# The state-space layer of a two-layer diffusion backbone: modulation sums in the other PSUM bank pair, back-rotations and transposes in other places

## The chip, the cores and the metric

The kernel runs on one core of a Trainium2 chip. The metric is the device time of one execution in microseconds (us). [...] Each engine takes its own instructions in order and waits at semaphores for the others.

## The reference

Two trunk layers run over 1024 latent tokens and 256 context tokens of width 1024. Layer 0 mixes tokens with differential attention, layer 1 with a bidirectional S5 state space; each mixer is followed by a squared-ReLU MLP, with RMS norms and modulation (shift, scale, gate) from `SiLU(c)` before and after. The change lies in layer 1's mixer:

```
def step(h, uc):
    bu = einsum('gpc,btgc->btgp', b_bar, uc)
    a_cum, hs = associative_scan(_linear_combine, (a, bu), axis=1)
    hs = hs + a_cum * h[:, None]
    y = real(einsum('gcp,btgp->btgc', c_mat, hs))
...
y = y_forward + y_backward[:, ::-1] + d_skip * h
g = gelu(y);  o1, o2 = split(g @ w_glu, 2);  out = o1 * sigmoid(o2)
```

There are 64 groups of 16 channels with 64 complex states each, scanned in both directions. The layer's modulation is `mod = SiLU(c) @ ada_w[1] + ada_b[1]`, a vector of six segments of 1024 for each of the two streams.

## The kernel before, in words

The program (class `Prog`) runs in stages: attention, output projection, MLP of layer 0, the state-space stage `s5()`, the gated linear unit `glu()`, and the MLP of layer 1. Most of the stages are ordered by a scheduler that estimates when each instruction is due. The main loop of `s5()` is written under `manual()`: TensorE, VectorE, ScalarE and GpSimd take their instructions in the order of the Python text. Only SyncE's DMA queue is still ordered by the scheduler.

Before the stage, token time is cut in chunks of 8 tokens, so that a scan runs over 160 chunks (32 of context, 128 of latent tokens). One step `n` of the loop (0 to 15) treats four groups of channels in both directions `d`:

- `inputs(n, d)` (L1765): 16 matmul calls into `xbank[d]`, the chunk inputs of the states. The two `xbank`s span PSUM banks 0 to 2 and share bank 1.
- `phase(n, d)` (L1744, GpSimd): adds two integer tables to the phases of the rotation; `trig(n, d)` (L1749 to L1753, ScalarE): five instructions make sines `Ps` and cosines `Pc` of them. The three phase buffers are used in turn, so `phase(n+1, 1)` writes where the sines of `(n, 0)` are, and `phase(n+1, 0)` where those of `(n-1, 1)` are.
- `rotate(n, d)` (L1774, VectorE, two instructions): multiplies `xbank[d]` by cosines (`t1`) and sines (`t2`); GpSimd adds the two (L1878 for `d` = 0, L1886 for `d` = 1). This turns the complex scan into real ones.
- `decay(n, d)` (L1779, ScalarE): fills `r`, in PSUM, with the decay; `scan(n, d)` (L1784, VectorE): two scans, over the two parts `c`, each of 320 elements.
- `back(engine, n, d, j)` (L1793): the rotation back, `j` = 0 with cosines and `j` = 1 with sines. For each direction VectorE does `j` = 0 and GpSimd `j` = 1.
- `outputs(n)`: `lags` (L1809), the terms inside a chunk, and `products` (L1817), the states times the output matrices, into `ypart(n, i)`. It is called one step later, as `outputs(n - 1)` in step `n`.
- For step `m = n - 2`, the GELU: square (L1860, ScalarE, reads `ybank(n)`), L1874 (VectorE), tanh (L1875), plus one (L1880), and the product with `y` (L1894, VectorE).
- `tr` (L1827): transposes of the result into `ypart(n, i)`; `tr_out`: ScalarE copies it rounded (L1832), VectorE stores the residue (L1833). Products in this kernel use such pairs of a rounded value and its residue.

`ybank(n)` is the pair of banks 4 and 5 for even `n`, 6 and 7 for odd `n`. `ypart(n, i)` takes the first half of each 256 elements; the second half is used by `accum(n, i)`, for the modulation. The framework sets its waits by whole banks: a matmul that writes a bank waits for readers of any part of it, and the other way round.

The modulation of layer 1, segments 2 to 5, is made in this stage in eight halves of 512 columns. List `mods` holds a triple (a, b, buffers) for each: in step a the weights are loaded (`ada_half_load`, four DMAs of 512 KB), in step b `ada_half_products` (L270) multiplies them into `accum(n)`, 64 rows of the profile, in step b + 1 ScalarE copies the sums (L1863), `ada_half_columns` (L274) transposes them into `accum(n, 1)`, and in step b + 2 `ada_half_add` (L279, L281, L284, VectorE) adds them to the table of modulations. Seven halves have b = 3, 5, ... 15; the eighth has b = 12.

Three more steps (16 to 18) finish outputs, GELU and transposes. Then `glu()` splits its weights (L137, L138) and multiplies (L132 to L134).

Of the kernel before, what the change touches and what calls it, by code (L numbers as in the profile page):

```python
# [9 lines left out]
AF = mybir.ActivationFunctionType  # L10
ALU = mybir.AluOpType
# [59 lines left out]
class Prog:  # L71
# [1627 lines left out]
    def s5(self):  # L1699
# [4 lines left out]
        v, act, pool, mm = nc.vector, nc.scalar, nc.gpsimd, nc.tensor.matmul  # L1704
# [8 lines left out]
        phs = [(self.fv(x, 2, 2, 160), self.fv(x + 2.5, 2, 160)) for x in (0, 7.5, 24.5)]  # L1713
        ts = [[(self.fv(x, 2, 2, 160), self.fv((12.5, 20)[d], 2, 2, 160)) for x in ((5, 29.5), (15, 17.5))[d]] for d in range(2)]
        cs = [[(self.fv(x, 2, 2, 128), self.fv(y, 2, 2, 128)) for x, y in (((5, 32), (29.5, 34)), ((15, 22.5), (17.5, 22.5)))[d]]
              for d in range(2)]
# [7 lines left out]

        extra = [self.view(self.U, 56, (2, 512)), self.fv(49, 2, 512), self.fv(53, 2, 512), self.wv(10, 2, 512)]
        early = [self.view(self.U, 4 * kk, (2, 512)) for kk in range(4)]
        mods = [(2 * i + 1, 2 * i + 3, extra) for i in range(7)] + [(8, 12, early)]

        def load_x(n):
            self.dma(slots[n % 2][3][:, 0:1024] if n else x_first, self.recd[n, :, 0:1024])  # L1730
# [9 lines left out]
        def phase(n, d):  # L1740

            x0, P = 32 * d + 2 * n, phs[(2 * n + d) % 3][0][:, 1].bitcast(I32)
            a, b = (At[:, x0 : x0 + 2], Bt[:, x0 : x0 + 2]) if n else (A0[:, d], B0[:, d])
            pool.tensor_tensor(P.rearrange("p x (a b) -> p x a b", b=16), bcast(a, 3, 16), bcast(b, 2, 10), ALU.add)  # L1744

        def trig(n, d):
            Ps, Pc = phs[(2 * n + d) % 3]
            P = Ps[:, 1].bitcast(I32)
            act.activation(Pc, P, AF.Sin, scale=0.5 * UNPHASE)  # L1749
            act.activation(Ps[:, 0], P, AF.Sin, scale=-UNPHASE)  # L1750
            act.activation(Ps[:, 1], P, AF.Sin, scale=UNPHASE)
            act.activation(Pc, Pc, AF.Square, scale=float(np.sqrt(2.0)))
            act.activation(Pc, Pc, AF.Copy, bias=-1.0)  # L1753
# [3 lines left out]
        def inputs(n, d):  # L1757
            X = slots[n % 2][0] if n else shaped(x_first, (2, 4, 128))
            cols = slice(0, 160) if d == 0 else slice(32, 192)
            for c in range(2):  # L1760
                for y in range(2):
                    o = 176 * (2 * c + y)
                    for h in range(2):
                        i = 2 * h + y
                        mm(xbank[d][64 * h : 64 * h + 64, o : o + 160], X[:, d, i, 64 * c : 64 * c + 64],  # L1765
                           U[:, 4 * n + i, cols], start=True, stop=True)

        def rotate(n, d):
            (Ps, Pc), (t1, t2) = phs[(2 * n + d) % 3], ts[d][n % 2]
            b = xbank[d]  # L1770
            for j, t in enumerate((t1, t2)):
                x = bass.AP(b.tensor, b.offset + (159 if d else 0) + 352 * j,
                            [list(b.ap[0]), [-352 if j else 352, 2], [176, 2], [-1 if d else 1, 160]])
                v.tensor_tensor(t, x, Ps if j else bcast(Pc, 1, 2), ALU.mult)  # L1774

        def decay(n, d):

            x0 = 32 * d + 2 * n
            act.activation(rx[:, :, 1:160], bcast(r8[:, x0 : x0 + 2], 2, 159), AF.Copy)  # L1779

        def scan(n, d):
            for c in range(2):
                t1, t2 = (t[:, c].rearrange("p x n -> p (x n)") for t in ts[d][n % 2])
                v.tensor_tensor_scan(t2, r, t1, 0.0, ALU.mult, ALU.add)  # L1784

        def back(eng, n, d, j):
            Ps, Pc = phs[(2 * n + d) % 3]
            o = cs[d][n % 2][j]
            if d:
                o = bass.AP(o.tensor, o.offset + 127, [list(o.ap[0]), [256, 2], [128, 2], [-1, 128]])  # L1790
            h = slice(31, 159)
            t2 = ts[d][n % 2][1][:, :, :, h]
            eng.tensor_tensor(o, t2, Ps[:, :, :, h] if j else bcast(Pc[:, :, h], 1, 2), ALU.mult)  # L1793
# [8 lines left out]
        def accum(n, i=0):  # L1802
            x = 2176 + 1024 * (n % 2) + 256 * i
            return self.PS[:, x : x + 128]
# [24 lines left out]
        def tr_out(kb, g, n):  # L1829
            b = ybank(n, (1, 128))  # L1830
            hi, lo = (shaped(gT[g][j][:, kb], (4, 128)) for j in range(2))
            act.activation(hi, b, AF.Copy, scale=0.5)  # L1832
            v.scalar_tensor_tensor(lo, b, 0.5, hi.bitcast(F32), ALU.mult, ALU.subtract)  # L1833
# [8 lines left out]
        with self.manual():  # L1842
            act.activation(U[:, :, 160:192], U[:, :, 0:32], AF.Copy)
            v.memset(rx[:, :, 0:1], 0.0)
            phase(0, 0)
            phase(0, 1)
            trig(0, 0)
            decay(0, 0)
            inputs(0, 0)
            inputs(0, 1)  # L1850
            load_x(1)
            load_w(1)
            for n in range(19):
                run, m = n < 16, n - 2
                gelu = 0 <= m < 16
                y, uf = ybank(n, (1, 128)), u.rearrange("p i t c -> p i (t c)")
                if 1 <= n <= 16:
                    back(pool, n - 1, 1, 1)
                if gelu:
                    act.activation(uf, y, AF.Square, scale=float(np.sqrt(0.044715)))  # L1860
                for a, b, w in mods:
                    if n == b + 1:
                        act.activation(self.adat[:, 0:128], accum(b), AF.Copy)  # L1863
                if run:
                    trig(n, 1)
                if 0 < n < 15:
                    phase(n + 1, 0)
                if run:
                    rotate(n, 0)
                for i, (a, b, w) in enumerate(mods):  # L1870
                    if n == b + 2:
                        self.ada_half_add(1, 2 + i // 2, i % 2, accum(n - 1, 1))
                if gelu:
                    v.scalar_tensor_tensor(uf, uf, 1.0, y, ALU.add, ALU.mult)  # L1874
                    act.activation(u, u, AF.Tanh, scale=float(np.sqrt(2.0 / np.pi)))  # L1875
                if run:
                    t1, t2 = ts[0][n % 2]
                    pool.tensor_tensor(t1, t1, t2, ALU.add)  # L1878
                if gelu:
                    act.activation(u, u, AF.Copy, bias=1.0)  # L1880
                if 0 < n < 15:
                    trig(n + 1, 0)
                if run:
                    rotate(n, 1)
                    t1, t2 = ts[1][n % 2]
                    pool.tensor_tensor(t1, t1, t2, ALU.add)  # L1886
                    scan(n, 0)
                    if n == 0:
                        phase(1, 0)
                        trig(1, 0)  # L1890
                    decay(n, 1)
                if gelu:
                    gv = ggs[m // 2 % 2].rearrange("p t g c -> p g t c")
                    v.tensor_tensor(gv[:, 4 * (m % 2) : 4 * (m % 2) + 4], u, ybank(n, (16, 8), (1, 16)), ALU.mult)  # L1894
                if run:
                    back(v, n, 0, 0)
                    back(pool, n, 0, 1)
                    scan(n, 1)
                    back(v, n, 1, 0)
                if n < 15:  # L1900
                    decay(n + 1, 0)
                if 1 <= n <= 16:
                    outputs(n - 1)
                if n < 15:
                    inputs(n + 1, 0)
                    inputs(n + 1, 1)
                if n + 1 < 16:
                    phase(n + 1, 1)
                if 3 <= n < 19:
                    tr((n - 3) // 2, 1 - n % 2, n)  # L1910
                    tr_out((n - 3) // 2, 1 - n % 2, n)
                for a, b, w in mods:
                    if n == b:
                        self.ada_half_products(w, accum(n))
                    if n == b + 1:
                        self.ada_half_columns(accum(n, 1))
                if n + 2 < 16:
                    load_x(n + 2)
                if 1 <= n and n + 1 < 16:
                    load_w(n + 1)  # L1920
                for i, (a, b, w) in enumerate(mods):
                    if n == a:
                        self.ada_half_load(w, 1, 2 + i // 2, i % 2)
# [402 lines left out]
```

## Time and profile before

| | |
|---|---|
| median of 3 runs | 2949.05 us (2947.05 to 2949.87) |
| profiled execution | 2948.53 us |
| its span | 2946.7 us |
| first `scan(0, 0)`, from the span's start | 1918.11 us |
| `scan(3, 0)` | 1947.28 us |
| `scan(15, 0)` | 2102.45 us |
| first matmul of `glu()` | 2127.05 us |
| mean granted TensorE clock | 0.981 |

In the rows of the profile, L12 is line 12 of the kernel. A group gives busy time, the mean of one instruction in ns, and the idle time of its engine just before it with what ended that. A row of the timeline gives start and length in us, engine, line, what is written and read, the count merged, and in brackets the idle time ahead and who ended it; where the engine named had long been done, it was another. The clock is a share of full speed.

### The profile page before, as it was taken

The numbers are of one execution on the slowest core, as the hardware profiler recorded it, in microseconds if no ns is written. First come the engines' busy times: TensorE is split into PE (matmuls) and PEld (weight loads), VectorE is DVE, ScalarE is ACT, GpSimd is POOL, SyncE is SP. The second block draws the span as 40 slices with busy tenths as digits, with TensorE's granted clock in tenths as the row PEclk, the third lists the DMA queues.
The fourth block names the chain that finished last, engine by engine and source line by source line (L and its number), as shares of the span: only waits on it lengthen the run. The fifth ranks groups of instructions, "written<-read, shape, count | busy, mean of one in ns | idle before, by whom it ended". The sixth has DMA issues, their size and how long they took to land.

```text
span 2946.7 us, 45520 instructions
## 1 busy us (share of the span) xinstructions
PE 2789.1 (95%) x16556; PEld 2300.8 (78%) x16556; DVE 1909.2 (65%) x2823; ACT 1304.4 (44%) x2476; POOL 990.9 (34%) x911
## 2 busy tenths in 40 slices
PE   7999999999899999999999999687799999999999
PEld 5687888888777877888777788576688778888887
DVE  5456888888764654444687754787633676659466
ACT  3325565555544743333432222355434655345443
POOL 2214667667653500000000002476301323327324
PEclk9999999999899999999999999889899999999999
DMA  9964444454716455322666653656534475467544
GB/s 265 296 193 159 136 157 154 147 154 156 239 59 187 136 159 169 121 97 88 211 191 187 181 158 95 170 182 184 178 115 154 149 228 188 150 214 268 161 136 140
DMA packets 404493, 494.42 MB, mean 168 GB/s; under 512 B 41014, under 2 KB 279596, under 8 KB 403372
## 3 DMA queue, kind: packets, MB, share of 16 engines
q1 hardware_dynamic: 403884, 489.42, 53.0%
q8 instruction: 130, 2.13, 0.3%
q10 hardware_dynamic: 384, 2.10, 0.3%
q14 instruction: 95, 0.78, 0.1%
HBM read 337.77 MB, written 149.43 MB: 165 GB/s over the span
## 4 chain that ended last, share of the span: by engine, by line
PE 66%; DVE 12%; DMA 7%; issue 6%; ACT 6%; POOL 2%; SPq 1%; DVEq 0%; ACTq 0%; POOLq 0%
PE PS L132 20%; PE PS L134 19%; PE PS L133 19%; ACT F L574 2%; DVE F L564 2%; PE PS L539 2%; PE PS L597 1%; DVE FD L1784 1%; DVE R L138 1%; SPq L80 1%; PE PS L208 1%; PE PS L1817 1%; DVE FD L1774 1%; DMA W<-in_mlp_w 1%; DVE FD L1675 1%
## 5 line engine op out<-in xcount | busy, mean ns | idle before, releaser
L132 PE MATMUL PS<-H,R 128*128 128x512 f32 (+1 forms) x816 | 301.8, 372 | 8.7 <-DVE FC L490 5.5
L132 PE MATMUL PS<-H 128*128 128x512 f32 x768 | 300.1, 392 | 3.6 <-ACT H L137 2.3
L133 PE MATMUL PS<-H 128*128 128x512 f32 x768 | 299.4, 390 | 0.0
L134 PE MATMUL PS<-H 128*128 128x512 f32 x768 | 298.7, 390 | 0.0
L133 PE MATMUL PS<-H,R 128*128 128x512 f32 (+1 forms) x816 | 293.3, 359 | 1.4 <-POOL H L138 1.4
L134 PE MATMUL PS<-H,R 128*128 128x512 f32 (+1 forms) x816 | 293.2, 360 | 0.0
L132 PE MATMUL PS<-R,H 128*128 128x512 f32 x540 | 216.7, 403 | 1.9 <-ACT R L137 1.6
L574 ACT ACTIVATE F<-F,stat 128x1280 f32<-128x1280 f32 x128 | 174.3, 1362 | 98.8 <-DVE F L564 98.5
L137 ACT ACTIVATE R<-W 128x512 fp32r<-128x512 f32 (+1 forms) x184 | 131.1, 717 | 189.7 <-PE PS L133 136.0
L133 PE MATMUL PS<-R,H 128*128 128x512 f32 x540 | 212.1, 393 | 0.0
L134 PE MATMUL PS<-R,H 128*128 128x512 f32 x540 | 211.6, 395 | 0.0
L138 DVE TENSOR_TENSOR H<-W,H 128x512 fp32r<-128x512 f32 (+1 forms) x145 | 136.5, 946 | 99.0 <-ACT H L137 93.5
L564 DVE TENSOR_SCALAR_CACHE_REDUCE F<-PS 128x1280 f32<-128x1280 f32 x128 | 185.1, 1482 | 14.1 <-PE PS L539 14.0
L138 DVE TENSOR_TENSOR R<-W,R 128x512 fp32r<-128x512 f32 (+1 forms) x148 | 126.3, 858 | 98.2 <-ACT R L137 77.8
L611 POOL TENSOR_SCALAR R<-F 128x256 fp32r<-128x256 f32 (+1 forms) x128 | 137.2, 1072 | 147.8 <-ACT F L610 134.4
L132 PEld LDWEIGHTS PS<-H,R 128*128 128x128 f32 x816 | 154.2, 189 | 38.8 <-DVE FC L490 7.2
L137 ACT ACTIVATE H<-W 128x512 fp32r<-128x512 f32 (+2 forms) x166 | 107.4, 653 | 170.6 <-PE PS L133 117.1
L539 PE MATMUL PS<-R,R 64*128 64x256 f32 (+1 forms) x1440 | 159.1, 349 | 16.6 <-DVE F L564 9.9
L134 PEld LDWEIGHTS PS<-H,R 128*128 128x128 f32 x816 | 154.2, 189 | 26.3 <-POOL R L138 1.4
L132 PEld LDWEIGHTS PS<-H 128*128 128x128 f32 x768 | 144.1, 188 | 37.1 <-ACT H L137 3.1
L133 PEld LDWEIGHTS PS<-H,R 128*128 128x128 f32 x816 | 154.6, 189 | 22.5 <-POOL H L138 1.6
L134 PEld LDWEIGHTS PS<-H 128*128 128x128 f32 x768 | 144.2, 188 | 30.2 <-issue 0.2
(460 smaller groups left out, 7172.7 us busy)
## 6 DMA issues: line engine op xcount, KB each, us to landing
W<-in_mlp_w SPq DMA_DIRECT2D x192, 256.0 KB
Ad<-F SPq DMA_DIRECT2D x112, 256.0 KB
W<-Ad SPq DMA_DIRECT2D x112, 256.0 KB
W<-in_ada_w SPq DMA_DIRECT2D x41, 512.0 KB
W<-in_mlp_w SPq DMA_DIRECT2D x32, 512.0 KB
H<-hidd SPq DMA_DIRECT2D x64, 256.0 KB
W<-in_s_w_glu SPq DMA_DIRECT2D x64, 256.0 KB
hidd<-FU SPq DMA_DIRECT2D x52, 256.0 KB
```

The lines of the kernel that those rows point to most:

```text
L80: return self.nc.sync.dma_start(out=out, in_=in_)
L132: mm(out, ah, bh, start=first, stop=False, **kw)
L133: mm(out, ah, bl, start=False, stop=False, **kw)
L134: mm(out, al, bh, start=False, stop=last, **kw)
L137: self.nc.scalar.activation(hi, src, AF.Copy)
L138: (lo_eng or self.nc.vector).tensor_tensor(lo, src, hi.bitcast(F32), ALU.subtract)
L208: self.nc.tensor.matmul(acc[32 * j : 32 * j + 32, 0:256], self.scT[:, 2 * k : 2 * k + 32], w[:, 256 * j : 256 * j + 256], start=k == 0, st ...
L539: mm(self.PS[:, o : o + k1 - k0], Q[rows, i, qs], K[j][rows, k0:k1], start=n == 0, stop=n == 2)
L564: ts(p[c], self.PS[:, 1280 * c : 1280 * c + 1280], 1.0, None, ALU.mult, ALU.min, accum_out=sm[:, c : c + 1])
L574: nc.scalar.activation(p[c], p[c], AF.Exp, bias=sm[:, c : c + 1], scale=-1.0, accum_out=sn[:, 0:1] if c else s0[:, u + 1 : u + 2])
L597: self.nc.tensor.transpose(tb[:, 128 * (kt - k0) : 128 * (kt - k0) + 128], w[:, 128 * kt : 128 * kt + 128], self.ident)
L611: nc.gpsimd.tensor_scalar(hi, t, 1.0, 0.0, ALU.mult, ALU.add)
```

## The change

- The modulation products of step b go into `accum(n - 1)`, the bank pair of the other parity; the copy, the transpose and the add follow (`accum(b - 1)`, `accum(n - 1, 1)`, `accum(n - 2, 1)`). On TensorE the transpose and the products now come after both `inputs`, in this order.
- The eighth half has b = 16 in place of 12, and its loads are in step 14 in place of 8.
- In ScalarE's order, `trig(n, 1)` comes ahead of the square and the copy of the sums; `decay(n + 1, 0)` comes after `tr_out`'s copy.
- The back-rotations change hands: GpSimd does `j` = 0, VectorE `j` = 1. VectorE's first stands between the two scans of direction 1, its second, of the step before, between the two halves of `rotate(n, 0)`.
- On GpSimd, the order stays: back-rotation, phase, addition, addition, back-rotation, phase. The two phase additions overwrite sines that VectorE's back-rotations now read.
- On TensorE the transposes come between `inputs(n + 1, 0)` and `inputs(n + 1, 1)`, which were together ahead of them.

```diff
@@ -1724,7 +1724,7 @@
 
         extra = [self.view(self.U, 56, (2, 512)), self.fv(49, 2, 512), self.fv(53, 2, 512), self.wv(10, 2, 512)]
         early = [self.view(self.U, 4 * kk, (2, 512)) for kk in range(4)]
-        mods = [(2 * i + 1, 2 * i + 3, extra) for i in range(7)] + [(8, 12, early)]
+        mods = [(2 * i + 1, 2 * i + 3, extra) for i in range(7)] + [(14, 16, early)]
 
         def load_x(n):
             self.dma(slots[n % 2][3][:, 0:1024] if n else x_first, self.recd[n, :, 0:1024])
@@ -1765,10 +1765,11 @@
                         mm(xbank[d][64 * h : 64 * h + 64, o : o + 160], X[:, d, i, 64 * c : 64 * c + 64],
                            U[:, 4 * n + i, cols], start=True, stop=True)
 
-        def rotate(n, d):
-            (Ps, Pc), (t1, t2) = phs[(2 * n + d) % 3], ts[d][n % 2]
+        def rotate(n, d, js=(0, 1)):
+            Ps, Pc = phs[(2 * n + d) % 3]
             b = xbank[d]
-            for j, t in enumerate((t1, t2)):
+            for j in js:
+                t = ts[d][n % 2][j]
                 x = bass.AP(b.tensor, b.offset + (159 if d else 0) + 352 * j,
                             [list(b.ap[0]), [-352 if j else 352, 2], [176, 2], [-1 if d else 1, 160]])
                 v.tensor_tensor(t, x, Ps if j else bcast(Pc, 1, 2), ALU.mult)
@@ -1778,8 +1779,8 @@
             x0 = 32 * d + 2 * n
             act.activation(rx[:, :, 1:160], bcast(r8[:, x0 : x0 + 2], 2, 159), AF.Copy)
 
-        def scan(n, d):
-            for c in range(2):
+        def scan(n, d, cs=(0, 1)):
+            for c in cs:
                 t1, t2 = (t[:, c].rearrange("p x n -> p (x n)") for t in ts[d][n % 2])
                 v.tensor_tensor_scan(t2, r, t1, 0.0, ALU.mult, ALU.add)
 
@@ -1855,28 +1856,30 @@
                 gelu = 0 <= m < 16
                 y, uf = ybank(n, (1, 128)), u.rearrange("p i t c -> p i (t c)")
                 if 1 <= n <= 16:
-                    back(pool, n - 1, 1, 1)
+                    back(pool, n - 1, 1, 0)
+                if run:
+                    trig(n, 1)
                 if gelu:
                     act.activation(uf, y, AF.Square, scale=float(np.sqrt(0.044715)))
                 for a, b, w in mods:
                     if n == b + 1:
-                        act.activation(self.adat[:, 0:128], accum(b), AF.Copy)
+                        act.activation(self.adat[:, 0:128], accum(b - 1), AF.Copy)
                 if run:
-                    trig(n, 1)
+                    rotate(n, 0, (0,))
+                if 1 <= n <= 16:
+                    back(v, n - 1, 1, 1)
                 if 0 < n < 15:
                     phase(n + 1, 0)
                 if run:
-                    rotate(n, 0)
+                    rotate(n, 0, (1,))
+                    t1, t2 = ts[0][n % 2]
+                    pool.tensor_tensor(t1, t1, t2, ALU.add)
                 for i, (a, b, w) in enumerate(mods):
                     if n == b + 2:
-                        self.ada_half_add(1, 2 + i // 2, i % 2, accum(n - 1, 1))
+                        self.ada_half_add(1, 2 + i // 2, i % 2, accum(n - 2, 1))
                 if gelu:
                     v.scalar_tensor_tensor(uf, uf, 1.0, y, ALU.add, ALU.mult)
                     act.activation(u, u, AF.Tanh, scale=float(np.sqrt(2.0 / np.pi)))
-                if run:
-                    t1, t2 = ts[0][n % 2]
-                    pool.tensor_tensor(t1, t1, t2, ALU.add)
-                if gelu:
                     act.activation(u, u, AF.Copy, bias=1.0)
                 if 0 < n < 15:
                     trig(n + 1, 0)
@@ -1893,27 +1896,28 @@
                     gv = ggs[m // 2 % 2].rearrange("p t g c -> p g t c")
                     v.tensor_tensor(gv[:, 4 * (m % 2) : 4 * (m % 2) + 4], u, ybank(n, (16, 8), (1, 16)), ALU.mult)
                 if run:
-                    back(v, n, 0, 0)
-                    back(pool, n, 0, 1)
-                    scan(n, 1)
-                    back(v, n, 1, 0)
-                if n < 15:
-                    decay(n + 1, 0)
+                    back(pool, n, 0, 0)
+                    scan(n, 1, (0,))
+                    back(v, n, 0, 1)
+                    scan(n, 1, (1,))
+                if n + 1 < 16:
+                    phase(n + 1, 1)
                 if 1 <= n <= 16:
                     outputs(n - 1)
                 if n < 15:
                     inputs(n + 1, 0)
-                    inputs(n + 1, 1)
-                if n + 1 < 16:
-                    phase(n + 1, 1)
                 if 3 <= n < 19:
                     tr((n - 3) // 2, 1 - n % 2, n)
                     tr_out((n - 3) // 2, 1 - n % 2, n)
+                if n < 15:
+                    inputs(n + 1, 1)
+                    decay(n + 1, 0)
+                for a, b, w in mods:
+                    if n == b + 1:
+                        self.ada_half_columns(accum(n - 1, 1))
                 for a, b, w in mods:
                     if n == b:
-                        self.ada_half_products(w, accum(n))
-                    if n == b + 1:
-                        self.ada_half_columns(accum(n, 1))
+                        self.ada_half_products(w, accum(n - 1))
                 if n + 2 < 16:
                     load_x(n + 2)
                 if 1 <= n and n + 1 < 16:
```

## The prediction

> **What bounds the kernel now.** I read the page first: engine totals, slices, granted clock.
>
> ```profile
> span 2946.7 us, 45520 instructions
> PE 2789.1 (95%) x16556; PEld 2300.8 (78%) x16556; DVE 1909.2 (65%) x2823; ACT 1304.4 (44%) x2476; POOL 990.9 (34%) x911
> PE   7999999999899999999999999687799999999999
> PEclk9999999999899999999999999889899999999999
> ```
>
> TensorE (PE) is busy 95% of the span, so only places where it pauses can give time. The low digits (slices 24 to 29 of 40, 73.7 us each) hold the state-space stage, and the clock row dips at the same place. Next, stretches from one scan(n,0) start to another: steps 1 to 3, steps 3 to 15, and the tail from step 15 to the first gated-linear-unit matmuls; the last row is a small piece inside a step.
>
> ```profile
> core 0: us, PE busy (x) PEld busy (x) DVE busy (x) ACT busy (x) POOL busy (x), PEclk, DMA share, GB/s
> 1947.20:2102.40 155.20, 123.57 (x1723) 108.12 (x1721) 124.01 (x171) 86.00 (x199) 92.59 (x71) 0.91 0.61 194
> 1929.30:1947.20 17.90, 17.80 (x232) 16.13 (x232) 17.37 (x24) 12.09 (x28) 15.74 (x13) 0.94 0.65 180
> 2102.40:2127.00 24.60, 15.85 (x202) 13.26 (x198) 11.46 (x19) 7.43 (x14) 4.48 (x3) 0.84 0.49 152
> 2020.30:2023.70 3.40, 3.31 (x24) 3.08 (x26) 3.40 (x6) 3.02 (x7) 2.77 (x2) 0.51 0.11 38
> ```
>
> Columns: length, busy time and count of PE, PEld, DVE, ACT, POOL, then granted clock, DMA share, GB/s. Steps 3 to 15 are 12 steps in 155.2 us, 12.93 each, in which no engine is full: PE 123.6 us, VectorE (DVE) 124.0, ScalarE (ACT) 86.0, GpSimd (POOL) 92.6. So the steps are bound by waits between engines. Steps 1 to 3, without modulation sums, have DVE busy 17.37 of 17.90. The groups of those 12 steps:
>
> ```profile
> L1774 DVE TENSOR_TENSOR FD<-PS,FD 128x640 f32<-128x640 f32 x49 | 38.0, 815 | 14.4 <-ACT FD L1753 14.4
> L1784 DVE TENSOR_TENSOR_SCAN FD<-PS,FD 128x320 f32<-128x320 f32 x48 | 36.6, 801 | 0.0
> L1793 DVE TENSOR_TENSOR FD<-FD 128x512 f32<-128x512 f32 x24 | 26.0, 1084 | 0.4
> L1833 DVE SCALAR_TENSOR_TENSOR H<-PS,H 128x512 fp32r<-128x512 f32 x12 | 8.3, 692 | 12.8 <-ACT H L1832 12.8
> L284 DVE TENSOR_TENSOR modc<-modc,ng 128x8 f32<-128x8 f32 x5 | 3.7, 737 | 0.2
> L1863 ACT ACTIVATE adat<-PS 128x128 f32<-128x128 f32 x7 | 1.9, 278 | 18.2 <-DVE FD L1874 9.2 <-PE PS L270 6.4 <-PE PS L274 2.5
> ```
>
> Reading: scans (L1784, four a step) never waited; DVE stood 14.4 us ahead of rotations (L1774) for ACT's trigonometry, and 12.8 us ahead of the transpose residue (L1833) for ACT's copy L1832. The back-rotations (L1793) average 1084 ns. The copy of modulation sums (L1863) kept ACT waiting 18.2 us. One step in order of time:
>
> ```profile
> 2008.22 0.28 ACT L1863 ACTIVATE adat<-PS 128x128 f32<-128x128 f32 x1 [2.31 <-DVE FD L1874]
> 2010.62 1.55 DVE L1774 TENSOR_TENSOR FD<-PS,FD 128x640 f32<-128x640 f32 x2 [2.41 <-ACT FD L1753]
> 2011.13 0.63 ACT L1880 ACTIVATE FD<-FD 128x512 f32<-128x512 f32 x1
> 2011.67 0.45 ACT L1749 ACTIVATE FD<-FD 128x320 f32<-128x320 int32 x1
> 2012.09 1.53 DVE L1784 TENSOR_TENSOR_SCAN FD<-PS,FD 128x320 f32<-128x320 f32 x2
> 2013.75 0.42 ACT L1779 ACTIVATE PS<-r 128x318 f32<-128x318 f32 x1
> 2013.76 1.28 POOL L1793 TENSOR_TENSOR FD<-FD 128x512 f32<-128x512 f32 x1
> 2014.11 1.48 DVE L1793 TENSOR_TENSOR FD<-FD 128x512 f32<-128x512 f32 x1
> 2015.51 1.52 DVE L1784 TENSOR_TENSOR_SCAN FD<-PS,FD 128x320 f32<-128x320 f32 x2
> 2017.07 0.69 DVE L1793 TENSOR_TENSOR FD<-FD 128x512 f32<-128x512 f32 x1
> 2017.13 0.44 ACT L1779 ACTIVATE PS<-r 128x318 f32<-128x318 f32 x1 [2.96 <-DVE FD L1784]
> 2017.50 0.58 ACT L1832 ACTIVATE H<-PS 128x512 fp32r<-128x512 f32 x1
> 2017.98 0.59 ACT L1860 ACTIVATE FD<-PS 128x512 f32<-128x512 f32 x1
> 2018.12 0.69 DVE L1833 SCALAR_TENSOR_TENSOR H<-PS,H 128x512 fp32r<-128x512 f32 x1 [0.35 <-ACT H L1832]
> 2020.26 0.68 DVE L1874 SCALAR_TENSOR_TENSOR FD<-FD,PS 128x512 f32<-128x512 f32 x1
> 2020.97 0.63 ACT L1875 ACTIVATE FD<-FD 128x512 f32<-128x512 f32 x1 [0.32 <-DVE FD L1874]
> ```
>
> ACT reaches the copy L1863 before the phases' sines, and waits until 2008.22; the five sine instructions follow, and DVE gets its phases only at 2010.62. The back-rotation at 2014.11, issued while GpSimd's (2013.76 to 2015.04) runs, takes 1.48; the one at 2017.07 takes 0.69. TensorE, around the same step:
>
> ```profile
> 2006.20 0.64 PE L270 MATMUL PS<-U,scT 128*32 128x128 f32 x16 [1.41 <-DVE H L1833]
> 2007.54 0.62 PE L270 MATMUL PS<-W,scT 128*32 128x128 f32 x16
> 2008.55 0.71 PE L1809 MATMUL PS<-W,U 128*128 128x128 f32 x4 [0.40 <-ACT adat L1863]
> 2013.81 2.39 PE L1765 MATMUL PS<-U,W 128*64 128x160 f32 x32
> 2016.13 0.66 PE L1827 MATMUL PS<-ident,U 128*128 128x128 f32 x4
> 2020.39 1.22 PE L1809 MATMUL PS<-H,U 128*128 128x128 f32 x4 [1.20 <-DVE modc L279]
> ```
>
> The 64 modulation matmuls (L270) start only after the transposes' residue, since they write the bank that DVE reads; the next outputs (L1809) wait in turn for the copy, or one step on for DVE's add (L279), each in the bank about to be written. At 2020.39 they take 1.22 instead of 0.71, in the stretch that the windows show at clock 0.51.
>
> **The change, part by part.**
>
> Modulation sums: in the other bank pair, the copy, columns and add are met by no output of their own step. The copy stands behind the sines and the square. The wait ahead of rotations, 14.4 us over the 12 steps, should go. What is late next is the square, L1860: it reads the bank in which the step before wrote its modulation products, so it can now wait for them; behind it on ACT stand the copy and, through L1874 on DVE, the tanh. PE's order decides that: outputs (2008.55 to 2013.81, 5.26), inputs (2.32), transposes (0.66), products (2006.20 to 2008.16, 1.96). Laid against the ring below, the products end about 1 us before the square is due. The columns and products now stand behind the second inputs; their readers, the copy and DVE's add, come a step later, so I cost the add's wait at nothing.
>
> Back-rotations: DVE's first goes between the two scans of the second direction, its second between the two halves of the first rotation. They are those that read the sines which GpSimd's next phase addition overwrites, so that addition waits for DVE, and GpSimd is quiet while DVE's runs. 24 times (1084 - 692) ns is 9.4 us off DVE. GpSimd's own back-rotation starts after its addition and ends 2.95 us after scan(n,0) starts (2015.04 - 2012.09), while DVE's now comes one scan (1.52 / 2) later than at 2014.11, 2.78 after it: a remainder of 0.1 to 0.2 each is left, and 0 if DVE is late. The phase additions that now wait have queued behind them GpSimd's next back-rotation or addition; the sines that need them come over 2 us later, so I cost them at nothing. With that cover gone each us late would be a us in the ring. The Trainium skill, "SBUF — State Buffer", section "Who interferes with whom", says that a VectorE instruction with two SBUF inputs and a GpSimd instruction that reads SBUF exclude each other and the one issued second waits for the whole first. The trace agrees: 2014.11 + 1.48 is 2015.59, 0.55 after GpSimd's end. By that rule alone the edit is worth the same 9.4 us less the remainder, 12 times 0.15, or 7.6.
>
> Transposes between the inputs, decay behind L1832: transposes start half of the 2.32 us inputs earlier, and ACT's copy no longer stands behind the decay, which waits for the last scan (2.96 at 2017.13). L1833's 12.8 us should go. New: the decay and the sines behind it now stand behind L1832, which waits for TensorE.
>
> First sum, DVE's ledger: 155.2 - 14.4 - 12.8 - 9.4 = 118.6 us. But that assumes that nothing takes their place. The tightest ring of dependences in the new order runs between ACT and DVE: sines (2011.67 to 2013.75) 2.08, square 0.59, L1874 0.68, tanh 0.63, the +1 copy (2011.13 to 2011.67) 0.54, sines of the next step 2.08, decay 0.42, scan 0.76, back-rotation 0.69, scan 0.76, decay 0.44, and again sines. That is 9.67; handing over costs 0.10 from DVE to ACT (2017.03 to 2017.13) and 0.04 the other way (2018.08 to 2018.12), twice each: 9.95. Overlap within ACT gives some back, and the remainder above takes about as much; I take 9.9 a step. TensorE's pair of steps is 2 x (5.26 + 2.32 + 0.66) + 1.96 and a column transpose (a quarter of 0.66), 18.6, so 9.3 a step at full clock. DVE's own busy time less 9.4 is 114.6, 9.55 a step. So the ring is the bound: 12 x 9.9 = 118.8. The small instructions behind the add of the columns (L284, 3.7 us in five) stay as they are and sit in the ring: 4. TensorE has 19.8 - 18.6 = 1.2 us to spare in a pair, less than the 1.7 us that a stretch of 3.4 at half clock costs; I allow one in two pairs at 1.5, 4.5 us. Sum 127.3 against 155.2: 28 us off.
>
> Steps 1 to 3 had DVE full and none of these stalls. The ring there is between 17.9 and 19.8; I put +1. The tail, 24.6 us:
>
> ```profile
> 2112.37 0.28 ACT L1863 ACTIVATE adat<-PS 128x128 f32<-128x128 f32 x1 [5.04 <-PE PS L270]
> ```
>
> There the copy held ACT for 5.04 us, with L1874's tanh behind it and the last outputs after it; that wait moves off them. Against it, the eighth half (before in steps 8 to 14) now has its products in step 16, copy and columns in 17 and add in 18: 1.96 us at full clock, 3.9 at half, partly beside other waits. Between -5 and +4; I take -1. Its four loads (2.1 MB, on SP's queue) move to step 14, and wait there for nothing that the rows show; the row of the tail has DMA at 0.49, and in the steps 0.61 x 155.2 / 127 is 0.75, so I cost them at 0, at most some 7 us if the weights after the stage came late. All else in the kernel only moves earlier.
>
> Total: -28 + 1 - 1 = -28. The profiled execution is its span 2946.7 plus 1.8 (2948.5), 0.5 under the median of 2949.05. From the median: **2921 us**.
>
> **The rivals.** First, TensorE comes late: the clock keeps falling to half, or the square waits for the modulation products. For it: 9.3 against 9.9 is little room, and the windows show 0.51 right after pauses (1.41 ahead of L270, 1.20 ahead of L1809). Against it: those pauses are the ones that the change removes. Were the mean clock still 0.91, 0.18 of some 130 us would run at half, 23 us, which costs 12; with the square late by 0.5 us in 8 steps that is 16 instead of 4.5: 2933 us. The Trainium skill, "TensorE: Matmul & The Clock Gate", section "A second HAM failure mode: psum-queue depth-cycling", speaks against the change here: where TensorE cycles through PSUM banks and stands idle often but briefly between groups of matmuls, the gate can swing between half and full. By that rule the 12 us would stay, and this rival's time with them. The trace so far shows half clock after longer pauses, not after short ones.
>
> Second, only the locks and the residue wait are saved, and the square takes the place of the copy as what waits for modulation: 14.4 stays. 36.6 - 14.4 is 22, less 4.5, less half of L1833's which then also follow TensorE: about 11 off, 2938 us.
>
> Third, slower: the clock. With TensorE asked for 9.3 us of every 9.9 instead of 123.6 of 155.2, the granted clock could stay low for long. A step is then 9.3 (1 + f) for a share f of work at half clock; it passes 12.93 at f = 0.39, and at f = 0.6 the 12 steps give 178.6, or 23 more: 2972 us. Against it: the page grants 9 in nearly every slice where PE is 9 busy.
>
> Last, none of the edited waits is at the end, since DMA loads that come later than DVE set the steps: 155.2 us at 194 GB/s. Against it: no wait for a load among these groups. About 2949.
>
> **How the numbers follow.** Forecast 0.62; TensorE late 0.22; sums still in the way 0.07; slower 0.05; nothing 0.04. The lowest sensible time is DVE's floor, 114.6 + 4: 36.6 off, with 5 in the tail 2908; the first rival's is 2933 and can be 3 worse. The range 2909 to 2936 leaves out the last three cases and a little of each end. About 0.2% (6 us) is what a measurement of this kernel can tell from no change. Faster takes the forecast, the first rival and nearly all of the second, 0.90; same 0.05; slower 0.05.
>
> **What would show it.** Scan starts 9.9 to 10.4 us apart from step 3 to 15 (11.3 in the few steps with stretched adds); DVE's L1793 mean under 800 ns; waits of L1774 for the sines and of L1833 for L1832 under 3 us each; new small waits of scans for the decay (0.3 each) and of L1874 for the square; PEclk in the stage near 0.98; PE over 90% busy there. A square that waits for L270 by over 1 us, or clock under 0.9, is the first rival. Step lengths near 12.9 would make the prediction wrong.

## The result and the profile after

The changed kernel takes 2917.78 us (median of 5 runs, 2916.40 to 2918.27) against 2949.39 for the kernel before beside it (5 runs, 2947.05 to 2953.54): a ratio of 0.989, 95% interval 0.9876 to 0.9905. The forecast was 2921, in a range of 2909 to 2936.

The page of the changed kernel, the rows that answer to those of before:

```profile
span 2914.8 us, 45549 instructions
PE 2772.2 (95%) x16556; PEld 2283.0 (78%) x16556; DVE 1895.8 (65%) x2823; ACT 1305.5 (45%) x2476; POOL 977.8 (34%) x911
PE   7999999999899999999999999869899999999999
```

In the rows PE, DVE, ACT, POOL and SP are TensorE, VectorE, ScalarE, GpSimd and SyncE. PS is PSUM, the memory to which all 16556 matmuls write; the program counts it in banks of 512 float32 values per partition. VectorE and ScalarE work on it too, while none of GpSimd's 911 instructions here reads or writes it.

The low digits in the 26th to 29th slice, 6877 before, are 8698 now. The same stretches of the stage, steps 3 to 15 in the second row, steps 1 to 3 in the first, and in the third the tail up to the gated linear unit's first matmuls and a little over (columns as before, granted clock third from the end):

```profile
1928.40:1947.80 19.40, 18.05 (x242) 16.18 (x241) 17.53 (x23) 11.97 (x28) 14.21 (x13) 0.97 0.60 172
1947.80:2072.00 124.20, 113.72 (x1690) 97.44 (x1686) 113.83 (x169) 87.11 (x198) 84.31 (x71) 1.00 0.81 245
2072.00:2095.00 23.00, 13.79 (x222) 11.57 (x223) 13.11 (x23) 9.13 (x17) 4.05 (x3) 0.89 0.39 123
```

Steps 3 to 15 take 124.2 us instead of 155.2, 10.35 each; TensorE and VectorE are both busy for 92% of it and the clock is full. The 31.9 us between the two spans divide as follows.

| part, us | before | after | difference |
|---|---|---|---|
| up to scan(0, 0) | 1918.1 | 1917.0 | -1.1 |
| step 0 | 11.2 | 11.5 | +0.3 |
| steps 1 to 3 | 17.9 | 19.3 | +1.4 |
| steps 3 to 15 | 155.2 | 124.2 | -31.0 |
| tail, to the first matmul of `glu()` | 24.6 | 21.7 | -2.9 |
| from there to the end | 819.7 | 821.1 | +1.4 |

So nearly the whole gain lies in the twelve steps. The groups in them (waits ahead of an instruction and what ended them stand at the end of a row; most lines of the changed kernel are up to 7 higher):

```profile
L1775 DVE TENSOR_TENSOR FD<-PS,FD 128x640 f32<-128x640 f32 x49 | 38.9, 814 | 0.0
L1785 DVE TENSOR_TENSOR_SCAN FD<-PS,FD 128x320 f32<-128x320 f32 x48 | 38.0, 812 | 4.2 <-ACT PS L1780 4.2
L1794 DVE TENSOR_TENSOR FD<-FD 128x512 f32<-128x512 f32 x24 | 17.4, 724 | 0.0
L1881 DVE SCALAR_TENSOR_TENSOR FD<-FD,PS 128x512 f32<-128x512 f32 x12 | 8.2, 682 | 3.5 <-ACT adat L1866 3.5
L1834 DVE SCALAR_TENSOR_TENSOR H<-PS,H 128x512 fp32r<-128x512 f32 x12 | 8.0, 666 | 0.0
L279 DVE TENSOR_TENSOR modc<-PS,modc 128x8 f32<-128x8 f32 x6 | 1.0, 167 | 2.5 <-ACT FD L1863 2.5
L1863 ACT ACTIVATE FD<-PS 128x512 f32<-128x512 f32 x12 | 7.0, 580 | 0.0
L1866 ACT ACTIVATE adat<-PS 128x128 f32<-128x128 f32 x6 | 1.6, 269 | 0.0
L1749 ACT ACTIVATE FD<-FD 128x320 f32<-128x320 int32 x24 | 10.9, 454 | 0.0
L1744 POOL TENSOR_TENSOR FD<-FD 128x320 int32<-128x320 int32 x23 | 16.8, 729 | 18.0 <-DVE FD L1794 18.0
```

Rotations (L1775) and the transposes' residue (L1834) no longer wait at all: 14.4 and 12.8 us are gone. Back-rotations (L1794) average 724 ns instead of 1084. In their place stand 4.2 us of scans that wait for the decay, 3.5 us of L1881 behind the square and the copy, and 2.5 us of the modulation add L279 behind the square. GpSimd's 18 us ahead of the phase additions cost nothing, for the sines that need the phases (L1749) never wait. Some rows of one step, in order of time:

```profile
2007.58 0.17 DVE L279 TENSOR_TENSOR modc<-PS,modc 128x8 f32<-128x8 f32 x1 [0.42 <-ACT FD L1863]
2009.73 1.53 DVE L1785 TENSOR_TENSOR_SCAN FD<-PS,FD 128x320 f32<-128x320 f32 x2
2011.47 1.28 POOL L1794 TENSOR_TENSOR FD<-FD 128x512 f32<-128x512 f32 x1
2011.66 0.42 ACT L1780 ACTIVATE PS<-r 128x318 f32<-128x318 f32 x1
2012.18 0.82 DVE L1785 TENSOR_TENSOR_SCAN FD<-PS,FD 128x320 f32<-128x320 f32 x1 [0.35 <-ACT PS L1780]
2012.92 0.67 DVE L1794 TENSOR_TENSOR FD<-FD 128x512 f32<-128x512 f32 x1
2013.67 0.73 POOL L1744 TENSOR_TENSOR FD<-FD 128x320 int32<-128x320 int32 x1 [0.92 <-DVE FD L1794]
```

VectorE's back-rotation at 2012.92 starts 0.17 us after GpSimd's has ended (2011.47 + 1.28 = 2012.75) and takes 0.67; GpSimd's phase addition waits for it. The scan at 2012.18 waits 0.35 for the decay. These are two links of the prediction's ring, seen from VectorE.

### The profile page after: what moved, and what is told of

It reads as the page before. It is cut to its first block, busy times and chain, and to the rows that moved or that the text cites. A ratio compares the mean times of both kernels' runs of the same rounds, so it can differ in the third digit from the quotient of the medians.

```text
span 2914.8 us, 45549 instructions
## 1 busy us (share of the span) xinstructions
PE 2772.2 (95%) x16556; PEld 2283.0 (78%) x16556; DVE 1895.8 (65%) x2823; ACT 1305.5 (45%) x2476; POOL 977.8 (34%) x911
## 4 chain that ended last, share of the span: by engine, by line
PE 66%; DVE 11%; ACT 8%; DMA 6%; issue 6%; POOL 3%; SPq 1%; DVEq 0%; ACTq 0%; POOLq 0%
PE PS L132 20%; PE PS L134 20%; PE PS L133 20%; ACT F L574 2%; PE PS L539 2%; DVE F L564 2%; PE PS L597 1%; DVE R L138 1%; DVE FD L1785 1%; PE PS L208 1%; DMA W<-in_mlp_w 1%; DMA W<-in_ada_w 1%; SPq L80 1%; DVE FD L1675 1%; DMA od<-FC 1%
## 5 line engine op out<-in xcount | busy, mean ns | idle before, releaser
L138 DVE TENSOR_TENSOR R<-W,R 128x512 fp32r<-128x512 f32 (+1 forms) x148 | 124.3, 845 | 101.1 <-ACT R L137 80.6
```

The costliest lines, as they stand in the source:

```text
L138: (lo_eng or self.nc.vector).tensor_tensor(lo, src, hi.bitcast(F32), ALU.subtract)
```

## The experiments

The theory: after the change, a ring between ACT and VectorE (sines, square, L1881, tanh, plus one, sines, decay, scan, back-rotation, scan, decay) sets a step at 9.9 us, with VectorE's own work and TensorE close behind. Rivals: TensorE or its clock is the bound; VectorE's own work is. All stretches below are steps 3 to 15, from scan(3, 0) to scan(15, 0), in each kernel's own trace: 155.2 us before, 124.2 after. A difference in steps is one trace against one. From the doubled decay on, each kernel was executed once, except the last, with both edits together.

**One part undone.** First the back-rotations:

```diff
-                    back(pool, n - 1, 1, 0)
+                    back(pool, n - 1, 1, 1)
...
-                if 1 <= n <= 16:
-                    back(v, n - 1, 1, 1)
...
-                    back(pool, n, 0, 0)
-                    scan(n, 1, (0,))
-                    back(v, n, 0, 1)
-                    scan(n, 1, (1,))
+                    back(v, n, 0, 0)
+                    back(pool, n, 0, 1)
+                    scan(n, 1)
+                    back(v, n, 1, 0)
```

> The changed kernel with the back-rotations as before (VectorE j = 0 after the scans, GpSimd j = 1). Theory of the ring (ACT and VectorE hand each other the work, 9.9 us a step): the 1.48 us back-rotation returns ahead of scan(n, 1), so a step is 0.5 longer and steps 3 to 15 take 130 instead of 124.2 us; VectorE's mean back-rotation goes to 1080 ns. Rival, TensorE is the bound: no change. Rival, VectorE's own work is the bound: 12 x 0.79 = 9.5 us more.

Measured: 129.0 us, 4.8 more; ratio to the kernel before 0.9924 (0.9908 to 0.9941). VectorE's back-rotations in this kernel:

```profile
L1794 DVE TENSOR_TENSOR FD<-FD 128x512 f32<-128x512 f32 x24 | 26.1, 1087 | 0.4
```

24 times (1087 - 724) ns is 8.7 us of VectorE's time, of which 4.8 show: VectorE's work is not alone the bound, and TensorE's is not either. The ring's 5.8 is within 1 us: steps of 10.0 now take 10.35 where 10.5 was expected. The clock is 0.96 here instead of 1.00, since it fell three times for 3.4 us; two of the steps concerned are no longer than their like, one is 0.5 longer.

Then the modulation sums, with ACT's new order kept:

```diff
-        ... + [(14, 16, early)]
+        ... + [(8, 12, early)]
...
-                        act.activation(self.adat[:, 0:128], accum(b - 1), AF.Copy)
+                        act.activation(self.adat[:, 0:128], accum(b), AF.Copy)
...
-                        self.ada_half_add(1, 2 + i // 2, i % 2, accum(n - 2, 1))
+                        self.ada_half_add(1, 2 + i // 2, i % 2, accum(n - 1, 1))
...
                 for a, b, w in mods:
+                    if n == b:
+                        self.ada_half_products(w, accum(n))
                     if n == b + 1:
-                        self.ada_half_columns(accum(n - 1, 1))
-                for a, b, w in mods:
-                    if n == b:
-                        self.ada_half_products(w, accum(n - 1))
+                        self.ada_half_columns(accum(n, 1))
```

> The changed kernel with the modulation sums in the bank pairs and steps of before (eighth half in steps 8 to 14), but with the sines still ahead of the square and the copy on ACT. Theory of the ring: outputs again wait for the copy, which stands behind the sines, and for VectorE's add; steps 3 to 15 take 133 us or a little more if the clock falls, 9 or more above 124.2; half-clock stretches come back. Rival, the gain came from the order on ACT alone: within 2 us of 124.2.

Measured: 134.6 us, 10.4 more, with the clock at 0.96; ratio 0.9943 (0.9928 to 0.9958). The waits of this kernel (engine and line that waited, for what, us in total, times, longest) have TensorE behind VectorE's add again, and ACT's copy and the residue behind late transposes:

```profile
ACT H L1833 <- PE PS L1828: 33.0, 12, 4.4
DVE H L1834 <- ACT H L1833: 14.6, 10, 2.7
PE PS L1810 <- DVE modc L279: 10.2, 7, 1.8
```

The last part as two kernels, since it moves two things. The transposes behind both inputs again:

```diff
                 if n < 15:
                     inputs(n + 1, 0)
+                    inputs(n + 1, 1)
                 if 3 <= n < 19:
                     tr((n - 3) // 2, 1 - n % 2, n)
                     tr_out((n - 3) // 2, 1 - n % 2, n)
                 if n < 15:
-                    inputs(n + 1, 1)
                     decay(n + 1, 0)
```

> The changed kernel with the transposes behind both inputs as before; the decay stays behind ACT's copy L1833. Theory of the ring: TensorE has room, the transposes may come 1.2 us later, nothing changes: 124.2 within 1 us. Rival, the place of the transposes is what removed the wait of the residue (12.8 us): steps 3 to 15 take 130 to 136 us.

Measured: 125.7 us, 1.5 more, and the whole 0.9888 (0.9874 to 0.9903) of the kernel before, the same as the change. Eleven steps differ by 0.3 us at most; one takes 11.0 us instead of 10.0. Ahead of the longer one TensorE paused, and its clock fell in the stretch behind that:

```profile
2027.48 0.71 PE L1810 MATMUL PS<-H,U 128*128 128x128 f32 x4 [1.51 <-DVE H L1834]
2028.12 3.60 PE L1818 MATMUL PS<-H,FD 64*128 64x128 f32 x32
```

```profile
2027.90:2031.40 3.50, 3.50 (x35) 3.38 (x33) 3.08 (x6) 2.61 (x6) 2.68 (x3) 0.57 0.71 167
```

The 32 products take 3.60 us where they take 2.06 at full clock. The traced execution is the longest of four (2918.02 us; the others take 2910.48 to 2912.22), so the step at half clock need not be in the others. So the transposes' new place is nearly free of effect on its own. At most it keeps TensorE's waits for the residue short: they are 10.4 us here, up to 1.7 each, against 4.3, up to 0.7.

The decay ahead of ACT's copy again:

```diff
                     inputs(n + 1, 0)
+                    decay(n + 1, 0)
                 if 3 <= n < 19:
...
                     inputs(n + 1, 1)
-                    decay(n + 1, 0)
```

> The changed kernel with decay(n + 1, 0) ahead of ACT's copy of the transposes as before; the transposes stay between the inputs. Theory of the ring: ACT's copy and with it the residue on VectorE come behind the last scan again, and the wait of the residue returns: steps 3 to 15 take 134 us, 9 above 124.2. Rival, the place of the transposes is what counts: within 1 us of 124.2.

Measured: 129.7 us, 5.5 more; ratio 0.9918 (0.9903 to 0.9933). The sign is the theory's, the size is half. The wait of the residue is back in full:

```profile
DVE H L1834 <- ACT H L1833: 12.9, 12, 1.1
```

Of that 12.9 the kernel shows 5.5. The changed kernel's waits behind the square, 3.5 us of L1881 and 2.5 of L279, are down to 0.2 in it, and VectorE's busy time is 1.8 less (112.0 against 113.8): 12.9 - 5.8 - 1.8 = 5.3. The forecast missed that the wait takes the place of others. The clock fell three times here too (0.96) and lengthened one step, by 0.3 us.

**One part alone, on the kernel before.** The modulation sums in the other banks and steps, with `[(14, 16, early)]`, `accum(b - 1)`, `accum(n - 2, 1)`, and

```diff
-                    if n == b:
-                        self.ada_half_products(w, accum(n))
-                    if n == b + 1:
-                        self.ada_half_columns(accum(n, 1))
+                    if n == b + 1:
+                        self.ada_half_columns(accum(n - 1, 1))
+                for a, b, w in mods:
+                    if n == b:
+                        self.ada_half_products(w, accum(n - 1))
```

> The kernel before with the modulation sums alone in the other bank pair and steps (b = 16 for the eighth), everything else as before, the copy still ahead of the sines on ACT. Theory: outputs no longer wait for the copy and the add, products no longer for the residue, so TensorE's pauses go and with them the half clock; steps 3 to 15 take 134 to 138 instead of 155.2 us, so this part alone gives more than half of the gain. Rival, the back-rotations and the order on ACT carry the gain: 145 us or more.

Measured: 134.1 us, 21.1 less than before; ratio 0.9946 (0.9929 to 0.9963).

```profile
1947.10:2081.20 134.10, 114.43 (x1672) 101.65 (x1672) 124.75 (x169) 85.60 (x198) 93.17 (x71) 0.96 0.71 224
```

VectorE is now busy 124.75 of 134.1, the clock is 0.96 instead of 0.91. The other two parts bring the remaining 10. The part holds the eighth half's move as well as the change of banks. The whole time is 14.7 us under that of the kernel before beside it (2930.23 against 2944.93), so the 21.1 of the one trace may be high. Undone one by one the parts give 4.8 + 10.4 + 1.5 + 5.5 = 22 of the 31 us: they overlap, and in the kernel with the decay moved back the trace shows how, one wait covering others.

**The bound of the new order.** The decay written twice, 0.4 us of ACT inside the ring:

```diff
                     decay(n, 1)
+                    decay(n, 1)
```

> The changed kernel with decay(n, 1) written twice, 0.4 us more on ACT in each step. Theory of the ring: the second one stands in it, 0.38 us a step: steps 3 to 15 take 128.5 to 129.5 instead of 124.2 us. Rivals, TensorE or VectorE's own work is the bound: 124.2 within 1 us.

Measured: 129.9 us, 5.7 more and a little over the forecast, though neither VectorE nor TensorE got any work:

```profile
1946.70:2076.60 129.90, 114.08 (x1690) 97.44 (x1686) 113.78 (x170) 92.32 (x210) 84.20 (x71) 1.00 0.78 234
```

```profile
DVE FD L1785 <- ACT PS L1780: 9.8, 12, 0.8
```

ACT's busy time rises by 5.2 and the steps by 5.7, nearly all of it in the scans that wait for the decay (9.8 instead of 4.2). That is the ring. TensorE against it, with every step's transposes made twice:

```diff
                     tr((n - 3) // 2, 1 - n % 2, n)
+                    tr((n - 3) // 2, 1 - n % 2, n)
```

> The changed kernel with each step's four transposes made twice, 0.6 us more on TensorE in each step. Theory of the ring: TensorE has 1.2 us to spare in a pair of steps, so nearly all is hidden: 124.2 to 126.5 us for steps 3 to 15. Rival, TensorE is the bound: 7 us more, 131.

Measured: 124.3 us. TensorE does 4.6 us more (118.36 against 113.72) and these steps do not move; the tail, outside them, takes 25.7 us instead of 21.7:

```profile
1944.60:2068.87 124.27, 118.36 (x1738) 102.72 (x1734) 113.92 (x170) 87.05 (x198) 84.26 (x71) 1.00 0.79 245
```

**The clock's share.** The kernel before, with a second set of inputs where TensorE waits for the residue:

```diff
                     tr_out((n - 3) // 2, 1 - n % 2, n)
+                if 3 <= n < 15:
+                    inputs(n + 1, 1)
```

> The kernel before with inputs(n + 1, 1) repeated after the transposes in steps 3 to 14, 1.16 us more on TensorE in the pause where it waits for the residue. Theory that part of the gain is the clock: the pauses become too short for the clock to fall, and steps 3 to 15 take 5 to 12 us less than 155.2 though TensorE does more. Rival, the clock cost nothing since TensorE is not at the end: 155 us or more.

Measured: 149.0 us, 6.2 less than before with some 14 us more to do (12 sets of 1.16):

```profile
1944.90:2093.90 149.00, 131.70 (x1913) 114.40 (x1912) 124.16 (x172) 85.91 (x199) 93.07 (x71) 0.97 0.67 202
```

The clock goes from 0.91 to 0.97. That fits a part of the 31 us being the cost of half clock, but the size is not settled: the whole takes 2942.76 us, 2.2 under the median of the kernel before beside it (2944.93, 2943.55 to 2951.95), and one execution of that kernel with the same mean clock, 0.985, took 2943.55.

**The eighth half** back in steps 8 to 14, in the new banks (`[(8, 12, early)]`):

> The changed kernel with the eighth half in steps 8 to 14 as before, in the new banks. Theory: its products, copy and add leave the tail, which falls by 2 us from 21.7, and cost 1 to 1.5 us in steps 12 to 14; together within 2 us of the changed kernel. Rival, the eighth half at the end is a part of the gain: 3 us or more slower.

Measured: 125.3 us for the steps (+1.1), 20.0 for the tail (-1.7), 2917.13 us in all. It is a move of about the same cost from one place to the other.

**Beyond the change.** Two edits that follow from the ring and from the four steps of 11.0 to 11.2 us. The first takes two ACT instructions out of the ring:

```diff
+                late = any(n == b + 1 for a, b, w in mods)
+                if gelu and not late:
+                    act.activation(uf, y, AF.Square, scale=float(np.sqrt(0.044715)))
                 if run:
                     trig(n, 1)
-                if gelu:
+                if gelu and late:
...
-                    trig(n + 1, 0)
+                    trig(n + 1, 0, last=False)
...
                     decay(n, 1)
+                if 0 < n < 15:
+                    trig_end(n + 1, 0)
```

Here `trig_end` is the last of the five instructions of `trig`, which `last=False` leaves out.

> The changed kernel with two ACT instructions out of the ring: the last of the five of trig(n + 1, 0) behind decay(n, 1), and, in steps without a copy of sums, the square ahead of trig(n, 1). Theory of the ring: 0.3 a step less, 121 us for steps 3 to 15 instead of 124.2, and no wait of the scan for the decay. Rivals, TensorE or VectorE's own work is the bound: 124 within 1 us.

Measured: 116.9 us, 7.3 less, more than the 3 expected; the whole, 2914.81 us, is only 1.8 under the changed kernel's traced execution (2916.63), in which the stage started 5.4 us earlier. Scans no longer wait for the decay. In two of the steps the small adds also came just ahead of GpSimd's addition (L284 at 0.17 us) and these steps fell from 11.0 to 9.3, which the ring does not say; without those two the saving is some 4.

The second puts the adds of the modulation columns between the halves of `rotate(n, 1)`:

```diff
-                for i, (a, b, w) in enumerate(mods):
-                    if n == b + 2:
-                        self.ada_half_add(1, 2 + i // 2, i % 2, accum(n - 2, 1))
...
-                    rotate(n, 1)
+                    rotate(n, 1, (0,))
+                for i, (a, b, w) in enumerate(mods):
+                    if n == b + 2:
+                        self.ada_half_add(1, 2 + i // 2, i % 2, accum(n - 2, 1))
+                if run:
+                    rotate(n, 1, (1,))
```

> The changed kernel with VectorE's adds of the modulation columns (L279, L281, L284) between the two halves of rotate(n, 1), where GpSimd has finished its addition. Theory: the four steps of 11.0 to 11.2 us are long because these 8-column instructions wait out GpSimd's 1.5 us addition; they fall to 10.0 to 10.4, and steps 3 to 15 take 119 to 121 instead of 124.2 us. Rival, these steps are long because of the add's chain itself (segments 2, 4 and 5 have more instructions): 124 within 1 us.

Measured: 119.6 us, 4.6 less (2911.03 us in all); the four steps take 10.1 to 10.3. The rows of L284 of the changed kernel and then of this one (shortest, median, longest in ns):

```profile
L284 DVE TENSOR_TENSOR modc<-modc,ng x4: 167/621/1079, 1965.8 to 2069.9; 128x8 f32<-128x8 f32 x4
```

```profile
L284 DVE TENSOR_TENSOR modc<-modc,ng x4: 168/168/168, 1964.9 to 2064.4; 128x8 f32<-128x8 f32 x4
```

In two of the four steps it is L284 that was long, in the other two L281 ahead of it. Eight columns cost 0.17 us alone and up to 1.08 while GpSimd adds. Both edits together:

> The changed kernel with the ring shortened (as in ring_shorter) and the small adds moved (as in adds_moved). Theory of the ring: both savings add up until VectorE's own work is the bound at 9.2 to 9.6 us a step; steps 3 to 15 take 115 to 118 instead of 124.2 us, and the whole 7 to 10 us less than the changed kernel. Rival, TensorE at 9.2 a step with its waits becomes the bound: 120 us or more.

Measured: 114.6 us for the steps, just under the forecast and 9.6 less than the changed kernel, and 18.1 instead of 19.3 for steps 1 to 3:

```profile
1945.90:2060.50 114.60, 113.34 (x1692) 97.53 (x1690) 110.88 (x169) 87.97 (x198) 84.30 (x71) 1.00 0.87 263
```

TensorE is busy 113.3 and VectorE 110.9 of 114.6, so little waiting is left; which of the two is now the bound was not tested. The median is 2909.01 us (2905.08 to 2914.49), 0.9871 of the kernel before (0.9854 to 0.9887). The trace shows its steps shorter than the change's; the two intervals overlap, so as a whole time that is not settled.

## Why the prediction was right

- **The bound.** That the twelve steps were bound by waits, not by an engine, holds: the instructions are the same, but for their order, the place of one half and which of two engines takes which back-rotation, and 31.0 us went. The slices were read one off: the low digits are the 26th to 29th, and the first of these ends at 1915 us, ahead of the first scan. The sum rests on stretches between scans and is not touched by that.
- **The ledger of VectorE**, 36.6 us of waits and locks, is gone nearly to the letter: 14.4 and 12.8 to zero, 8.6 of 9.4 of the lock. Of the remainder, about 0.1 us a step is there, at the back-rotation between the halves of the rotation (0.78 us against 0.67 between the scans).
- **The ring.** 9.9 a step was forecast; eight of the twelve steps take 9.9 to 10.0, the four with stretched adds 11.0 to 11.2. Doubling the decay lengthens it, more TensorE work does not. Its two small waits are the forecast's: 0.35 a step ahead of a scan, and behind the square 0.4 (L279, put at nothing) or 0.6 (L1881). The sum left out the copy of the sums: in six steps L1881 starts when that has ended, 0.27 us after the square. That the ring, 118.8, and VectorE's ledger, 118.6, gave the same number is chance. The measured time does not choose between them; the doubled decay and the shorter ring do.
- **The small adds**, 4 us: 4 x 1.1, and the steps with the adds moved are 4.6 shorter. The forecast named L284 alone; in two of the four steps it is L281.
- **The allowance for TensorE**, 4.5 us for stretches at half clock, was the term that was too large: the clock is 1.00 there. Less 0.8 that the ring and 0.6 that the adds took beyond their terms, that is the 3 us between the 28 forecast for these steps and the 31.0 measured. The first rival's square did not wait for modulation products.
- **Steps 1 to 3**: +1 forecast, +1.4 measured. **The tail**: -1 forecast, -2.9 measured; the eighth half costs there about what it saves in the steps.
- **"All else only moves earlier"** was not exact: from the gated linear unit on, the trace has 1.4 us more. Over all the kernels here that part takes 816.9 to 823.0 us, so this is not told from the difference between executions.
- **The transposes' place** was put down as a reason why the residue's wait goes. It is hardly one: with the transposes back, 1.5 of 12.8 us return. With the decay ahead of ACT's copy 12.9 do, so the decay's place is the reason.
- **The rivals.** The clock that stays low: refuted, 1.00. The Trainium skill, "TensorE: Matmul & The Clock Gate", section "A second HAM failure mode: psum-queue depth-cycling", says that the gate swings between half and full where TensorE pauses often and briefly between groups; here the clock stays full though TensorE's groups wait 12 times for VectorE:

```profile
PE PS L1810 <- DVE H L1834: 4.3, 6, 0.7
PE PS L1828 <- DVE FD L1897: 3.2, 3, 1.5
PE PS L1828 <- DVE U L1897: 2.4, 3, 1.4
```

  One pause of 1.51 us in the kernel with the transposes undone was followed by half clock, so the length of a pause does not tell the two apart; the last section has what does better.
- **The other rivals.** Sums still in the way: refuted by the waits of the copy and of the square, both 0.0. DMA as the bound: refuted, the queue moved 245 GB/s instead of 194 and no group waits for a load in these steps.

## What to carry to other kernels

Where no engine is full, list the waits of the fullest one, find for each what its releaser stands behind, and then add up the tightest ring of dependences in the new order: no step can be shorter than that sum, however many waits are removed. Side work that shared PSUM banks with the main work here made TensorE, ACT and VectorE wait for each other; put it in the bank that nobody touches in that step. Undo the parts of a change one by one before giving a part the credit.

## What the runs showed of the hardware

VectorE and GpSimd exclude each other also for tiny instructions: L284 on 8 columns took 0.17 us alone and 1.08 while GpSimd's 1.5 us addition ran. The Trainium skill, "SBUF — State Buffer", section "Who interferes with whom", says this for two SBUF inputs, and the trace agrees. It says too that `tensor_scalar`, which has one, can contend in the modes that use both ports; the trace agrees here as well:

```profile
L281 DVE TENSOR_SCALAR modc<-modc x2: 1079/1084/1090, 2047.6 to 2068.8; 128x8 f32<-128x8 f32 x2
```

With the adds moved, the same instruction takes 0.17.

The granted clock changes only at multiples of 3.41 us in these records, so each such stretch can be set against the next. In steps 3 to 15 of the 14 traces the clock fell to half 23 times, and each time TensorE had been busy for at most 0.56 of the stretch before. Of the 470 stretches after which it stayed full, 10 were as low. The lowest of the changed kernel is 0.67. So how full a stretch is tells more than how long one pause is, though it does not settle every case. In the one trace of the kernel before with repeated inputs, some 14 us of useless matmuls went with 6 us less in these steps; the whole times do not confirm that.
